# Output projection of the last eight token chunks as 2x2 block products with seven products per pair

## The chip, the cores and the metric

The kernel runs on one core of a Trainium2 chip. The metric is device time in microseconds of one execution, the median of three runs. The core has TensorE (PE in the profile; its weight loads are the row PEld), VectorE (DVE), ScalarE (ACT), GpSimd (POOL) and the queue engine SyncE (SP), which issues nearly all DMAs.

## What is computed

One encoder layer on 2048 tokens of width 1024, in fp32. The input is projected once; half of the columns feed a bidirectional gated linear attention (GLA), the other half a latent attention (MLA) with a dense softmax; the outputs of both, 512 columns each, are gated, put side by side and go through one output projection, a residual and a layer norm:

```python
def hybrid_mixer(x, positions, w_in, ..., w_out):
    h = x @ w_in
    ...
    o_a = gla_branch(g_q, g_k, g_v, g_gate, g_lr_f, g_lr_b, ...)
    o_b = mla_branch(m_cq, m_ckv, m_kr, m_gate, positions, ...)
    return jnp.concatenate([o_a, o_b], axis=-1) @ w_out

x = layer_norm(DEEPNORM_ALPHA * x + mixed, ln_g, ln_b)
```

The change concerns `@ w_out`, a product of 2048x1024 by 1024x1024, and the residual and norm behind it.

## The kernel before

All products keep fp32 accuracy by splitting each operand into a rounded high part ("hi", made by ScalarE, line L370) and a remainder ("lo", line L376, by GpSimd or VectorE). `mm3` (L422) then adds three matmuls: high by high (L424), high by low (L425), low by high (L426).

The tokens are cut into 16 chunks of 128. The program has three stages. **Sweep A** (`sweep_a`, 21.75 us per step) does the first half of the input projection and GLA chunk by chunk, **sweep C** the rest of the projection and the other scan direction. **Attention** (`attention`) goes over 16 blocks of 128 queries, transposed so that queries lie on the free axis. The order of its instructions is written out as a table of places (`PLACE`, `PLACE_OUT`): every step of each block is put at a place, all are sorted by it, and `in_order` makes each engine keep that order.

The **output projection** (`OutProj`) is the end of the program. The eight row blocks k of w_out, each 128x1024, are fetched, split and kept in SBUF (`W[k]`, tiles woh and wol). For a chunk c:

- `load` issues four DMAs of 256 KB: the GLA half of the row block (`of` from oa_s), its MLA half (`of` from ob_s) and two factors for the MLA half, the gate (`gr` from gm_s) and the reciprocal softmax sum (`gr` from r_s, broadcast over partitions). There are two `gr` tiles, used in turn.
- `gate` multiplies the MLA half by both factors on GpSimd (two operations of 128x512), `hi` and `lo` split both halves into oh and ol.
- `product` makes 48 matmuls of 128x512: two halves n of the columns, eight k, three matmuls each. The results stand in PSUM: odd chunks in a tile of two banks (po), even ones in two single banks (pmb, px).
- `residual` reads a bank with VectorE (L1983: alpha times x plus the product) and takes statistics (L1984); `finish` forms mean and variance (L1992, L1993), the normalisation by VectorE in two halves (L1995), six small ScalarE operations for the reciprocal root (L1997 to L2002), scale and shift (L2004) and two output stores (L2005).

The product of the last chunk is made by `last_product` in pieces of 512, 256 and 256 columns, so that reading can follow closely. Chunks 0 to 3 are interwoven with the last attention blocks; from chunk 4 on the order is that of the loop at the end of `attention`: in pass c the residual input of the next chunk is fetched, chunk c+2 is split, chunk c+4 loaded and chunk c multiplied and finished. Four steps of the last query block stand inside it: behind chunk 5's product its softmax sums (sx on TensorE, `rc` on VectorE), behind chunk 7's product the transposed reciprocals (`turn`: rt on TensorE, in the bank ap), the last value product (`y`, in the bank o) and their ScalarE copies (`rows`, `yc`) with stores to r_s and ob_s, from which chunks 12 to 15 are loaded.

Of the kernel before, what the change touches and what calls it, by code (L numbers as in the profile page):

```python
# [18 lines left out]
P = 128  # L19
S = 2048  # L20
# [16 lines left out]
LATE_GATES = (NCH - 1, NCH - 2, 0)  # L37
STORE_POOL = (0, 1)
# [86 lines left out]
    sum=(38.16, 49.19),  # L125
)
# [233 lines left out]
class K:  # L360
# [138 lines left out]
    def run(self):  # L499
        tc, nc, ins = self.tc, self.nc, self.ins  # L500
        with ExitStack() as top:
# [12 lines left out]
            self.ob_s = [dp.tile([P, H, QB], F32, name=f"ob_s{b}") for b in range(NQB)]  # L514

# [26 lines left out]
            rp = top.enter_context(tc.tile_pool(name="res", bufs=1, side="right", reuse_waits="tile"))  # L542
            self.ckvT_h = rp.tile([P, NKT, P], F32R, name="ckvT_h")
            self.ckvT_l = rp.tile([P, NKT, P], F32R, name="ckvT_l")
            self.kr = rp.tile([P, NKT, P], F32R, name="krs")
            self.vh = rp.tile([P, NKT, P], F32R, name="vh")
            self.vl = rp.tile([P, NKT, P], F32R, name="vl")
# [64 lines left out]
    def sweep_a(self):  # L612
        tc, nc, ins, cp = self.tc, self.nc, self.ins, self.cp
        with ExitStack() as ctx:
# [55 lines left out]
            g1 = ctx.enter_context(tc.tile_pool(name="g1", bufs=1))  # L670

# [7 lines left out]
            def step(i, steps):  # L679

                def after(g, k):
                    for n, d in steps.get((g, k), ()):
                        run(n, i if d == "cur" else i - 1)
                for g in range(3):
                    for k in self.products(ch[i], g, after):
                        pass
                    after(g, NK - 1)
                if i and ch[i]["c"] not in LATE_GATES:
                    for k in self.gate_products(ch[i]["c"], *ch[i]["x"], ip):
                        after(3, k)  # L690
                    self.gate_end(ch[i]["c"], g1)
# [17 lines left out]
            for i in range(4, NCH):  # L709
                if ch[i]["c"] > 0:  # L710
# [89 lines left out]
    def ga_x(self, i):  # L800
# [7 lines left out]
        self.lo(xl[:, :, 0], xf, xh[:, :, 0], "dve" if i < 4 else "pool")  # L808
# [228 lines left out]
    def ga_av(self, d):  # L1037
# [9 lines left out]
        nc.scalar.activation(oi, Op[:, :, 1], AF.Copy)  # L1047
# [5 lines left out]
    def ga_state(self, d):  # L1053
# [20 lines left out]
        if c > 0:  # L1074
            G.tensor_tensor(Sb[up], Sb[up], Us[up], ALU.add)
# [20 lines left out]


# [428 lines left out]
    def attention(self):  # L1526
# [4 lines left out]
        with ExitStack() as ctx:  # L1531
# [262 lines left out]
            for c, o in enumerate(first):  # L1794
# [4 lines left out]
                put(end + out["gate"][c], op.gate, o)  # L1799
            for c in range(2):  # L1800
# [26 lines left out]

            with fixed():
# [16 lines left out]
            for c in range(4, NCH):  # L1845
                with fixed():
                    if 4 < c < NCH - 1:
                        op.load_res(rest[c + 1])
                    split(c + 2)
                    load(c + 4)  # L1850
                    op.product(rest[c])
                    op.finish(rest[c])
                with self.after(*last.values()), fixed():
                    for f in {4: (tot, oh, ol), 5: (tsum, rcp), 7: (turn, y, rows, yc)}.get(c, ()):
                        f(nb - 1)


class OutProj:
# [3 lines left out]
    def __init__(self, kern, ctx, qp, bp, sp, ps, pa, pb, pc, pd):  # L1862
# [3 lines left out]
        self.raw, self.W, self.gr = {}, {}, {}  # L1866
# [24 lines left out]
    def load_ln(self):  # L1891
        self.ln = [self.slot(n) for n in ("lng", "lnb")]
        for t, n in zip(self.ln, ("ln_g", "ln_b")):
            self.nc.sync.dma_start(t, self.k.ins[n].rearrange("p (a d) -> p a d", a=2))

# [35 lines left out]
    def banks(self, o):  # L1931

        c = o["c"]
        if c < 2 or c % 2:
# [12 lines left out]
    def product(self, o):  # L1947
        if o["c"] == NCH - 1:
            return self.last_product(o)
# [8 lines left out]

    def last_product(self, o):

        c = o["c"]
        tiles = [self.ps.tile([P, 2, 512], F32, tag="pS", name=f"po{c}")[:, 0]]
        tiles += [p.tile([P, 512], F32, tag=t, name=f"p{t}{c}") for p, t in self.single[2:]]
        o["rr"] = self.bp.tile([P, 2, 512], F32, tag="ph", name=f"rr{c}", bufs=3)
        o["bn"] = self.sm.tile([P, 3, 6], F32, tag="bn3", name=f"bn{c}")
        f2 = lambda t: t.rearrange("p a d -> p (a d)")
        for i, cs in enumerate((slice(0, 512), slice(512, 768), slice(768, 1024))):
            ps = tiles[i][:, :cs.stop - cs.start]
            for k in range(NK):
                wh, wl = self.W[k]  # L1970
                self.k.mm3(ps, o["oh"][k // 4][:, k % 4], o["ol"][k // 4][:, k % 4], wh[:, cs], wl[:, cs],
                           start=(k == 0), stop=(k == NK - 1))
            rr = f2(o["rr"])[:, cs]
            self.nc.vector.scalar_tensor_tensor(rr, f2(o["xr"])[:, cs], ALPHA, ps, ALU.mult, ALU.add)
            self.nc.vector.bn_stats(o["bn"][:, i], rr)
# [10 lines left out]
    def finish(self, o):  # L1986
        kern, nc, sm = self.k, self.nc, self.sm
# [6 lines left out]
        for n in range(2):  # L1994
            V.scalar_tensor_tensor(rr[:, n], rr[:, n], mv[:, 0:1], self.ln[0][:, n], ALU.subtract, ALU.mult)  # L1995
# [6 lines left out]
        Ac.activation(rs, t, AF.Copy, scale=y)  # L2002
        for n in range(2):
            V.scalar_tensor_tensor(rr[:, n], rr[:, n], rs, self.ln[1][:, n], ALU.mult, ALU.add)  # L2004
# [69 lines left out]
```

## Time and profile before

| | |
|---|---|
| median of three runs | 1290.73 us (1290.65 to 1293.42) |
| profiled execution | 1291.78 us, span 1290.0 us |
| granted TensorE clock | 0.999 |
| chunk 4's product begins | 1149.4 us |
| chunk 8's product begins | 1194.24 us |
| last matmul | 1281.5 us |
| end of the span | 1290.0 us |

The span runs from the first to the last instruction; the 1.78 us between it and the execution's time lie around it. A row of the timeline gives the start, the duration, engine, line, operation, result and operands, shape, count, and in brackets the idle time ahead of it with what ended it. The durations of matmuls are latencies that overlap; the distance between two starts is what one costs. In DMA rows of SP the duration is the time to issue; the landing comes later.

### The profile page before, as it was taken

To read this page: it belongs to the slowest core of one execution; us is meant where nothing else is said; L and a number is where in the kernel's file an instruction comes from. 1 tells how busy PE (TensorE), PEld (TensorE's weight loads), DVE (VectorE), ACT (ScalarE), POOL (GpSimd) and SP (SyncE) were. 2 spreads that over 40 slices of the span, in tenths; PEclk is the share of its full clock that TensorE was granted. 3 is DMA by queue.
4 is the path that set the end of the run, shared out by engine and by line. 5 is a ranking of instruction groups with operands and counts; after the bars stand their busy time and mean duration, and the time that the engine had idled before them with its cause. 6 is when DMAs were issued, how large, how long until landed. Compare 5 with 4: busy or idle time off the path is not lost.

```text
span 1290.0 us, 19998 instructions
## 1 busy us (share of the span) xinstructions
PE 1265.4 (98%) x6988; PEld 1118.1 (87%) x6988; DVE 921.0 (71%) x1678; ACT 840.9 (65%) x1482; POOL 791.2 (61%) x500
## 2 busy tenths in 40 slices
PE   7999999999999999999999999999999999999997
PEld 7999998999889999999788888888888888888886
DVE  6865665555675555555898888888888889469655
ACT  7765656555676556655688888888888888523221
POOL 0243232232567666671288888889999999946550
PEclk9999999999999999999999999999999999999999
DMA  8232322232565555565401111122223110367752
GB/s 288 73 92 58 91 58 76 65 84 65 190 216 181 187 196 180 194 213 167 138 1 41 42 41 41 41 58 61 63 74 104 45 42 9 123 204 234 240 171 73
DMA packets 113444, 145.81 MB, mean 113 GB/s; under 512 B 17494, under 2 KB 70110, under 8 KB 113344
## 3 DMA queue, kind: packets, MB, share of 16 engines
q1 hardware_dynamic: 105184, 142.42, 35.3%
q0 software_dynamic: 768, 2.10, 0.5%
q8 instruction: 55, 0.90, 0.3%
q10 hardware_dynamic: 7392, 0.03, 0.3%
q14 instruction: 45, 0.37, 0.1%
HBM read 94.14 MB, written 50.36 MB: 112 GB/s over the span
## 4 chain that ended last, share of the span: by engine, by line
PE 87%; ACT 3%; DVE 2%; POOL 2%; issue 1%; DMA 1%; SPq 0%; DVEq 0%; ACTq 0%; POOLq 0%
PE o L426 4%; PE o L424 4%; PE pS L1560 4%; PE o L425 4%; PE pS L1561 4%; PE pS L1562 4%; PE pS L1563 4%; PE pS L1564 4%; PE ipa L424 3%; PE ipa L426 3%; PE ipa L425 3%; PE pz L425 2%; PE po L426 2%; PE po L425 2%; PE po L424 2%; PE pz L424 2%
## 5 line engine op out<-in xcount | busy, mean ns | idle before, releaser
L376 POOL TENSOR_TENSOR pl<-s,ph 128x1024 fp32r<-128x1024 f32 x128 | 306.1, 2415 | 56.7 <-ACT ph L370 56.7
L1582 DVE TENSOR_TENSOR rm<-pS,rm 128x512 f32<-128x512 f32 x210 | 144.7, 689 | 26.5 <-ACT s L1569 20.9
L1606 DVE TENSOR_TENSOR s<-s,mb 128x1024 f32<-128x1024 f32 x128 | 151.1, 1212 | 9.4 <-PE mb L1600 9.3
L1569 ACT ACTIVATE s<-pS 128x1024 f32<-128x1024 f32 x128 | 131.2, 1025 | 37.8 <-PE pS L1564 33.7
L370 ACT ACTIVATE ph<-s 128x1024 fp32r<-128x1024 f32 x128 | 134.9, 1057 | 13.5 <-PE o L426 12.9
L1610 ACT ACTIVATE s<-s 128x1024 f32<-128x1024 f32 x128 | 131.4, 1050 | 13.4 <-DVE s L1606 13.3
L424 PE MATMUL ipa<-wah,xah 128*128 128x384 f32 (+1 forms) x384 | 129.9, 338 | 6.7 <-ACT wah L370 6.7
L1069 POOL TENSOR_TENSOR Us<-Us,cw 128x512 f32<-128x512 f32 x16 | 18.6, 1163 | 181.7 <-DVE Us L1067 166.2
L425 PE MATMUL ipa<-wal,xah 128*128 128x384 f32 (+1 forms) x384 | 124.7, 325 | 0.2 <-DVE wal L376 0.2
L426 PE MATMUL ipa<-wah,xal 128*128 128x384 f32 (+1 forms) x384 | 124.7, 325 | 0.0
L1560 PE MATMUL pS<-qh,ckvT_h 128*128 128x512 f32 x256 | 102.5, 401 | 0.8 <-DVE rm L1582 0.4
L424 PE MATMUL o<-ph,vh 128*128 128x512 f32 x256 | 101.1, 395 | 0.0
L1561 PE MATMUL pS<-ql,ckvT_h 128*128 128x512 f32 x256 | 99.9, 390 | 0.0
L1562 PE MATMUL pS<-qh,ckvT_l 128*128 128x512 f32 x256 | 99.9, 390 | 0.0
L1563 PE MATMUL pS<-rh,krs 128*128 128x512 f32 x256 | 99.9, 390 | 0.0
L1564 PE MATMUL pS<-rl,krs 128*128 128x512 f32 x256 | 99.8, 390 | 0.0
L426 PE MATMUL o<-ph,vl 128*128 128x512 f32 x256 | 99.8, 390 | 0.0
L425 PE MATMUL o<-pl,vh 128*128 128x512 f32 x256 | 99.7, 389 | 0.0
L1633 DVE TENSOR_TENSOR ap<-ap,s 128x512 f32<-128x512 f32 x120 | 83.1, 693 | 3.5 <-ACT s L1610 0.8
L424 PEld LDWEIGHTS ipa<-wah,xah 128*128 128x128 f32 x384 | 72.9, 190 | 7.6 <-ACT wah L370 7.0
L376 POOL TENSOR_TENSOR ol<-of,oh 128x512 fp32r<-128x512 f32 x32 | 43.4, 1356 | 53.2 <-ACT oh L370 53.2
L424 PE MATMUL pz<-xch,wzh 128*128 128x256 f32 x256 | 74.8, 292 | 0.0
(327 smaller groups left out, 3836.9 us busy)
## 6 DMA issues: line engine op xcount, KB each, us to landing
xcf<-xT_dram SPq DMA_DIRECT2D x16, 512.0 KB, 4.8
xr<-x_dram SPq DMA_DIRECT2D x16, 512.0 KB, 5.8
out_dram<-rr SPq DMA_DIRECT2D x32, 256.0 KB, 4.5
xaf<-xT_dram SPq DMA_DIRECT2D x14, 512.0 KB, 3.8
oib<-oi_s SPq DMA_DIRECT2D x16, 256.0 KB, 3.9
qdb<-qd_s SPq DMA_DIRECT2D x16, 256.0 KB, 5.3
SU<-su_s SPq DMA_DIRECT2D x16, 256.0 KB, 4.7
ub<-u_s SPq DMA_DIRECT2D x16, 256.0 KB, 4.2
```

The costliest lines, as they stand in the source:

```text
L370: return nc.scalar.activation(dst, src, AF.Copy).ins
L376: return e.tensor_tensor(dst, src, hi.bitcast(F32), ALU.subtract).ins
L424: mm(out, ah, bh, start=start, stop=False)
L425: mm(out, ah, bl, start=False, stop=False)
L426: mm(out, al, bh, start=False, stop=stop)
L1560: mm(ps[:, e], kh, qh, start=True, stop=False)
L1561: mm(ps[:, e], kh, ql, start=False, stop=False)
L1562: mm(ps[:, e], kl, qh, start=False, stop=False)
L1563: mm(ps[:, e], kr, rh, start=False, stop=False)
L1564: mm(ps[:, e], kr, rl, start=False, stop=True)
L1582: V.tensor_tensor(d["rm"], src[:, e], d["rm"], ALU.max)
L1606: V.tensor_tensor(s, s, d["mb"][:, None, :].to_broadcast([P, 2, QB]), ALU.subtract)
```

## The change

Chunks 8 to 15 are taken two at a time (class `Pair`). Rows 0 and 1 of the block matrix A are the two chunks (the odd one is row 0), its columns the GLA and the MLA half; B is w_out cut into four blocks of 512x512. Instead of eight block products of 128x512x512 (96 matmuls) the pair makes seven (84 matmuls) in Winograd's form, with the sums

- S1 = A21 + A22, S2 = S1 - A11, S3 = A11 - A21, S4 = A12 - S2 of the tokens (four VectorE operations per pair),
- T1 = B12 - B11, T2 = B22 - T1, T3 = B22 - B12, T4 = B21 - T2 of the weights.

The products are P1 = A11 B11, P2 = A12 B21, P3 = S4 B22, P4 = A22 T4, P5 = S1 T1, P6 = S2 T2, P7 = S3 T3, each into a bank of its own (four single banks in turn). P1 and P7 are also copied by ScalarE, and VectorE adds the copies to P6 in PSUM (U2, U3), then reads each result out of several banks:

```diff
+    product=dict(P1=0.0, P5=2.72, P6=5.44, P3=8.16, P7=10.88, P2=13.6, P4=16.32),
+    last=dict(P1=0.0, P5=2.72, P6=5.44, P3=8.16, P2=10.88, P7=13.6, P4=16.32),
...
+    def add(self, n):
+        out, x, y, f = dict(S1=lambda: (self.s1, a21, a22, ALU.add), S3=lambda: (a21, a11, a21, ALU.subtract),
+                            S2=lambda: (a11, self.s1, a11, ALU.subtract), S4=lambda: (a11, a12, a11, ALU.subtract))[n]()
+        self.nc.vector.tensor_tensor(out, x, y, f)
...
+    def weights(self, n, k):
+        if n in ("P5", "P6", "P7"):
+            return self.op.wt(dict(P5=1, P6=2, P7=3)[n], k)
+        wk, cs = dict(P1=(k, 0), P2=(k + 4, 0), P3=(k + 4, 1), P4=(k, 1))[n]
+        return [w[:, cs * 512:(cs + 1) * 512] for w in W[wk]]
...
+    def copy(self, ps):
+        self.nc.scalar.activation(self.cp, ps(), AF.Copy)
+    def sum(self, ps):
+        self.nc.vector.tensor_tensor(ps(), ps(), self.cp, ALU.add)
+    def read(self, r, n, ps, first, cs=slice(0, 512)):
+        rr = o["rr"][:, n, cs]
+        if first:
+            self.nc.vector.scalar_tensor_tensor(rr, o["xr"][:, n, cs], ALPHA, ps(), ALU.mult, ALU.add)
+        else:
+            self.nc.vector.tensor_tensor(rr, ps(), rr, ALU.add)
...
+        for n, r, h, x, first in (("R1", 0, 0, 0, True), ("R5", 1, 1, 1, True), ("R6", 0, 1, 3, True), ("R5b", 0, 1, 1, False),
+                                  ("R2", 0, 1, 2, False), ("R3", 1, 1, 2, False), ("R7", 0, 0, b["P2"], False),
+                                  ("R4b", 1, 0, 2, last)) + (() if last else (("R4", 1, 0, 3, True),)):
```

**Weights.** In steps 4 to 14 of sweep A, 16 blocks of w_out (128x512, 256 KB) are loaded, 16 subtractions made on GpSimd (behind its Sb addition, and ahead of xal), 16 roundings on ScalarE (behind its oi copy), 16 remainders on GpSimd, and 32 stores of 256 KB to DRAM. Attention fetches them back: T1 and the high part of T2 (3 MB) behind the last scores, into tiles whose last reader has gone; the low part of T2 and the high part of T3 (2 MB) behind chunk 5's residual input; the low part of T3 (1 MB) at chunk 6; T4 (2 MB) behind chunk 7's product, over the right halves of the first four weight blocks.

```diff
+        w = self.wt[k, t] = self.cb.tile([P, 512], F32, tag="raw", name=f"wb{t}_{k}", bufs=4)
+        n = 512 * (int(t[1]) - 1)
+        self.nc.sync.dma_start(w, self.ins["wO"][k + 4 * (int(t[0]) - 1)][:, n:n + 512])
...
+        with self.after(self.oi_act):
...
+                    self.hi(h, wt[k, n[1]])
+                    self.nc.sync.dma_start(self.wt_s[int(n[1])][0][:, k], h.bitcast(F32))
...
+        with self.after(self.sb_last):
...
+                    i = G.tensor_tensor(wt[k, "1"], b["12"], b["11"], ALU.subtract)
...
+                    i = G.tensor_tensor(t, wt[k, n[1]], halves.pop(0).bitcast(F32), ALU.subtract)
+                    self.nc.sync.dma_start(self.wt_s[int(n[1])][1][:, k], t.bitcast(F32))
...
+        with self.after(*([self.wt_last] if hasattr(self, "wt_last") else [])):
+            self.lo(xl[:, :, 0], xf, xh[:, :, 0], "dve" if i < 4 else "pool")
...
+            for j, t in enumerate(("1h", "1l", "2h")):
+                put(end + 1.2 + 0.01 * j, op.fetch_t, t)
...
+                op.fetch_t("2l")
+                op.fetch_t("3h")
...
+            put(1.0, op.fetch_t, "3l")
+            put(21.9, op.fetch_t, "4h")
+            put(21.91, op.fetch_t, "4l")
```

**Chunks 6 and 7.** From chunk 6 on the order comes from places again. The four steps of the last query block that stood behind chunk 7's product now stand at 5.4 to 6.5 us after chunk 6's start, between its two halves of columns. Chunk 7 uses the banks o and ap. ln_g and ln_b are copied by ScalarE into PSUM, and the SBUF tiles that held them (named lng and lnb) become the row blocks `of` of pairs 1 and 3, so DMAs into "lnb" and "lng" are loads of chunks 10 and 11. The norm is divided in `finish_a` and `finish_b`, with the same operations.

```diff
+            for place, f in ((5.4, turn), (5.41, y), (6.5, rows), (6.51, yc)):
+                put(place, f, nb - 1)
+            put(2.0, op.ln_psum, 0)
+            put(3.5, op.ln_psum, 1)
...
-                    for f in {4: (tot, oh, ol), 5: (tsum, rcp), 7: (turn, y, rows, yc)}.get(c, ()):
...
     def banks(self, o):
+        if c == PAIR0 - 1:
+            return [p.tile([P, 512], F32, tag=t, name=f"p{t}{c}") for p, t in self.single[2:]]
...
-    def last_product(self, o):
```

On GpSimd, where chunks 8 and 9 were split, the rows were (of is the row block, gr its factors, oh and ol the parts):

```order
L376 TENSOR_TENSOR ol8_0_12931<-of8_12738,oh8_0_12929 128x512
L1916 TENSOR_TENSOR of8_12738<-of8_12738,gr4_12583 128x512 x2
L376 TENSOR_TENSOR ol8_1_12937<-of8_12738,oh8_1_12935 128x512
L376 TENSOR_TENSOR ol9_0_13025<-of9_12838,oh9_0_13023 128x512
L1916 TENSOR_TENSOR of9_12838<-of9_12838,gr5_12593 128x512 x2
L376 TENSOR_TENSOR ol9_1_13031<-of9_12838,oh9_1_13029 128x512
```

Now they are, for pair 0 (chunks 9 and 8), with the last digit of a name the pair's number:

```order
L1996 TENSOR_TENSOR of9_12988<-of9_12988,gr5_12739 128x512 x2
L398 TENSOR_TENSOR A11l0_13159<-of9_12988,A11h0_13117 128x512
L398 TENSOR_TENSOR S1l0_13222<-s1_0_13197,S1h0_13202 128x512
L398 TENSOR_TENSOR S2l0_13228<-of9_12988,S2h0_13224 128x512
L1996 TENSOR_TENSOR lnb_12572<-lnb_12572,gr4_12729 128x512
L398 TENSOR_TENSOR S3l0_13264<-of8_12888,S3h0_13261 128x512
L1996 TENSOR_TENSOR lnb_12572<-lnb_12572,gr4_12729 128x512
L1996 TENSOR_TENSOR lng_12571<-lng_12571,gr5_12739 128x512 x2
L398 TENSOR_TENSOR A22l0_13320<-of8_12888,A22h0_13268 128x512
L398 TENSOR_TENSOR A12l0_13338<-of9_12988,A12h0_13259 128x512
L398 TENSOR_TENSOR S4l0_13344<-of9_12988,S4h0_13266 128x512
```

The gates of the next pair's chunks (lnb, lng) stand ahead of the last three remainders of this pair. On ScalarE the copies rt15 and yc15 stood behind chunk 7's norm:

```order
L2001 ACTIVATE ln7_t_13101<-ln7_w_13102 128x1
L2002 ACTIVATE ln7_r_13103<-ln7_t_13101,ln7_y_13100 128x1
L1711 ACTIVATE rt15_13120<-rt15_13114 4x128
L1734 ACTIVATE yc15_13123<-y15_13116 128x512
L370 ACTIVATE oh10_0_13128<-of10_12939 128x512
```

They now stand behind chunk 5's norm, the two copies of the norm's vectors and the first rounding of pair 0:

```order
L2263 ACTIVATE ln5_r_13058<-ln5_t_13056,ln5_y_13055 128x1
L2144 ACTIVATE ln0_13112<-lng_12571 128x1024
L2144 ACTIVATE ln1_13115<-lnb_12572 128x1024
L392 ACTIVATE A11h0_13117<-of9_12988 128x512
L1783 ACTIVATE rt15_13153<-rt15_13119 4x128
L1806 ACTIVATE yc15_13156<-y15_13121 128x512
L392 ACTIVATE S1h0_13202<-s1_0_13197 128x512
```

They moved from two chunks later, and have a row ahead of them that reads chunk 9's load. At the end of VectorE's order (pw0 to pw3 are the single banks, xr holds the sum of a row block), behind the last whole bank of the pair, it now says:

```order
L2036 TENSOR_TENSOR pw2_13274<-pw2_13274,pc3_14009 128x512
L2044 TENSOR_TENSOR xr14_13793<-pw2_13274,xr14_13793 128x512
L2042 SCALAR_TENSOR_TENSOR xr14_13793<-xr14_13793,pw2_13274 128x512
L2044 TENSOR_TENSOR xr14_13793<-pw3_13275,xr14_13793 128x256
L2050 BN_STATS bn14_14027<-xr14_13793 128x6 x2
L2269 SCALAR_TENSOR_TENSOR xr15_13770<-xr15_13770,ln15_r_13990,ln1_13115 128x512 x2
L2044 TENSOR_TENSOR xr14_13793<-pw0_13272,xr14_13793 128x256
```

The last row reads the last quarter of the result; before, nothing of another chunk stood between the last pieces.

More of the change, by code (lines that the diff above doesn't have):

```diff
@@ L514, in run @@
             self.ob_s = [dp.tile([P, H, QB], F32, name=f"ob_s{b}") for b in range(NQB)]
+            self.wt_s = {j: [dp.tile([P, 4, 512], F32, name=f"wt{j}{p}_s") for p in "hl"] for j in range(1, 5)}
             ident = cp.tile([P, P], F32, name="ident")
@@ L709, in sweep_a @@
             for i in range(4, NCH):
+                for k, t in WT_LOADS.get(i, ()):
+                    self.wt_load(k, t)
                 if ch[i]["c"] > 0:
@@ L1826, in split @@
                     op.lo(rest[c], 1)
+            pairs = [Pair(op, p, PAIR0 + 2 * p + 1, PAIR0 + 2 * p) for p in range((NCH - PAIR0) // 2)]
             with fixed():
@@ new lines, in attention @@
+            for place, f in ((5.4, turn), (5.41, y), (6.5, rows), (6.51, yc)):
[5 more added lines that the diff above has]
+            put(21.91, op.fetch_t, "4l")
+            for q in pairs:
+                q.put(put, 4 * half + PAIR_US * q.p, q is pairs[-1])
+            for _, _, fn, a in sorted(todo, key=lambda e: e[:2]):
+                with self.in_order(late):
+                    fn(*a)
```

239 lines of the change are left out of this document (205 added, 34 removed).

## The prediction

> **What bounds the kernel now.** I read the page first: the busy shares and the chain of work that ended last.
>
> ```profile
> PE 1265.4 (98%) x6988; PEld 1118.1 (87%) x6988; DVE 921.0 (71%) x1678; ACT 840.9 (65%) x1482; POOL 791.2 (61%) x500
> PE 87%; ACT 3%; DVE 2%; POOL 2%; issue 1%; DMA 1%; SPq 0%; DVEq 0%; ACTq 0%; POOLq 0%
> ```
>
> TensorE is busy for 98% of the span and is 87% of the chain, so matmuls that go are worth time where they are issued back to back. The list of what TensorE waited for, from 1080 us to the end (total, times, longest), and the busy time by stretches (PE, PEld, DVE, ACT, POOL, then clock, DMA share, GB/s) say that they are:
>
> ```profile
> PE y L424 <- DVE rc L1692: 0.3, 1, 0.3
> 1170.00:1180.00 10.00, 10.00 (x47) 8.05 (x46) 8.24 (x15) 3.02 (x9) 7.84 (x6) 1.00 0.40 118
> 1190.00:1200.00 10.00, 10.00 (x46) 8.15 (x45) 9.62 (x14) 3.44 (x11) 6.39 (x5) 1.00 0.91 318
> 1205.10:1226.88 21.78, 21.78 (x97) 18.02 (x97) 13.42 (x20) 5.30 (x16) 10.68 (x9) 1.00 0.70 224
> ```
>
> There is one wait of 0.3 us in 210 us, at clock 1.00. But look at the neighbours: VectorE has 9.62 of 10 us filled and the DMA engines a share of 0.91 at 1190, just where the pairs are prepared. TensorE is never late only because everything is ahead of it; the change puts more on all of them and gives them less time.
>
> **The matmuls that go.** The timeline of TensorE, first matmul of chunk 8, first of chunk 9, and two of the last quarter:
>
> ```profile
> 1194.24 0.39 PE L424 MATMUL pmb<-woh,oh 128*128 128x512 f32 x1
> 1205.14 0.39 PE L424 MATMUL po<-woh,oh 128*128 128x512 f32 x1
> 1281.37 0.28 PE L425 MATMUL pap<-wol,oh 128*128 128x256 f32 x1
> 1281.49 0.28 PE L426 MATMUL pap<-woh,ol 128*128 128x256 f32 x1
> ```
>
> 48 matmuls take 10.90 us, 0.2271 each (the 0.39 is latency, not pitch). A pair has 84 instead of 96: 4 x 12 x 0.2271 = 10.90 us. The narrow matmuls (pitch 0.12) are 24 instead of 48, and each two cost 0.24 against 0.227: 0.16 more. **-11.06 us.**
>
> **Sweep A.** Eleven steps get three operations each on GpSimd (the last one two), up to three roundings on ScalarE, and DMAs of 256 KB.
>
> ```profile
> 307.25 2.39 POOL L376 TENSOR_TENSOR xal<-xaf,xah 128x1024 fp32r<-128x1024 f32 x1 [3.29 <-ACT xah L370]
> 304.25 0.60 ACT L1516 ACTIVATE gs<-ipg 128x512 f32<-128x512 f32 x1 [2.20 <-PE ipg L426]
> 281.75:303.50 21.75, 21.75 (x139) 20.73 (x138) 11.75 (x23) 12.76 (x28) 6.83 (x6) 1.00 0.26 73
> PE Ap L425 <- DVE qbl L376: 1.1, 1, 1.1
> ```
>
> The new work stands in the gap of 3.29 us on GpSimd (three operations of about 1.3, so 0.6 too much) and in that of 2.20 us on ScalarE (three of about 0.6). DMAs use 0.26 of the engines. What may be late is xal, by about 1 us, and the lines of VectorE beside it; TensorE waited there once for qbl, 1.1 us. Value **+0.3**, bounds 0 and 1.5. The three fetches of 1 MB after the last scores have SP's empty stretch to themselves:
>
> ```profile
> 1057.00 30.64 SPq L1735 DMA_DIRECT2D ob_s<-yc  x2
> 1098.89 0.33 SPq L1873 DMA_DIRECT2D wof<-wO_dram  x1
> ```
>
> From 1087.6 to 1098.9 there are 11.3 us; 3.1 MB at the 318 GB/s above take 9.9. Nothing is charged; without that cover it would be about 1 us on a weight that is needed much later.
>
> **The softmax row moved into chunk 6.** It now stands behind the first half of chunk 6, which ends where px begins; it needs rc.
>
> ```profile
> 1177.11 0.39 PE L424 MATMUL px<-woh,oh 128*128 128x512 f32 x1
> 1179.89 0.18 DVE L1694 RECIPROCAL rc<-rc 128x4 f32<-128x4 f32 x1
> ```
>
> rc is done at 1180.07; TensorE is there at 1177.11 and stands still: **+3.0**. VectorE's order up to there is unchanged, so I see nothing that brings rc forward; two fetches of 1 MB, ahead of the output stores whose buffers VectorE reuses, may delay it (bounds 2.5 and 4.5).
>
> **Chunk 7's banks.** Chunk 7 now uses the o and ap banks, which hold rt and y until ScalarE has copied them; on ScalarE the copies stand behind A11h0, and that waits for chunk 9's first transfer. Its issue, the median landings between 1160 and 1215 us, and the copies as they are now:
>
> ```profile
> 1182.66 0.33 SPq L1907 DMA_DIRECT2D of<-oa_s  x1
> 1184.28 0.53 SPq L1910 DMA_DIRECT2D of<-ob_s  x1
> of<-oa_s SPq DMA_DIRECT2D x6, 256.0 KB, 3.9
> of<-ob_s SPq DMA_DIRECT2D x6, 256.0 KB, 7.5
> 1198.18 0.25 ACT L1711 ACTIVATE rt<-rt 4x128 f32<-4x128 f32 x1
> 1198.34 0.57 ACT L1734 ACTIVATE yc<-y 128x512 f32<-128x512 f32 x1
> ```
>
> Landing 1186.6, A11h0 about 0.6, copies 0.7: 1187.9. TensorE ends chunk 6 at 1180.07 + 0.81 (rt and y) + 5.45 = 1186.3. **+1.6**, bounds 0.5 and 3. Behind yc stands the store of ob_s, and behind that on SP, also behind 1 MB of wt3, are the loads of pair 1: 1188 instead of 1189.78 for chunk 10 today, yet now two chunks at once.
>
> **The fourth product of pair 0 (P3) waits for S4l0.** On GpSimd S4l0 stands behind the gates of chunk 11, so pair 0 waits for pair 1's load. Gates (two at a time) and remainders cost:
>
> ```profile
> 1177.39 2.66 POOL L1916 TENSOR_TENSOR of<-of,gr 128x512 f32<-128x512 f32 x2
> 1191.48 3.44 POOL L1916 TENSOR_TENSOR of<-of,gr 128x512 f32<-128x512 f32 x2
> 1195.67 1.29 POOL L376 TENSOR_TENSOR ol<-of,oh 128x512 fp32r<-128x512 f32 x1 [0.74 <-ACT oh L370]
> 1180.79 1.84 POOL L376 TENSOR_TENSOR ol<-of,oh 128x512 fp32r<-128x512 f32 x1 [0.74 <-ACT oh L370]
> ```
>
> Chunk 9's last part lands at 1184.28 + 7.5 = 1191.8, its gates end at 1194.5 to 1195.2; only then are chunk 11's gate buffers free. Its ob_s goes out 1.2 later, at 1195.7 to 1196.4, lands 7.5 later at 1203.2 to 1203.9, is gated by 1205.9 to 1207.3, and A22l0, A12l0, S4l0 (3 x 1.29 to 1.84) end at 1209.8 to 1212.8. TensorE begins pair 0 at 1187.9 + 10.9 = 1198.8 and is at P3 36 matmuls later, 1207.0. That is 2.8 to 5.8 us; the extra 1.3 MB (wt3, ob_s) in the queue is worth another 4.1 at 318 GB/s, and a landing like that of oa_s (3.9) would leave nothing. I take **+5.0**, bounds 0 and 10.
>
> Pair 1: its P3 is due at 1198.8 + 19.08 + 5.0 + 8.2 = 1231.1. Chunk 13's slot comes free with S4l0 near 1212; eight issues (4.3), 7.5, gates 3.1 and three remainders 4.2 give 1231.1 too: **+1.0**, bounds 0 and 4. Later pairs have an emptier queue.
>
> **VectorE in the pairs.** The groups between 1205 and 1248.6, which hold four chunks (busy total, mean ns), and the longest such row of the tail:
>
> ```profile
> L2004 DVE SCALAR_TENSOR_TENSOR rr<-rr,ln_r,lnb 128x512 f32<-128x512 f32 x8 | 9.8, 1264 | 1.6 <-ACT ln_r L2002 1.6
> L1995 DVE SCALAR_TENSOR_TENSOR rr<-rr,mv,lng 128x512 f32<-128x512 f32 x8 | 5.6, 745 | 0.0
> L1983 DVE SCALAR_TENSOR_TENSOR rr<-xr,px 128x512 f32<-128x512 f32 x2 | 1.4, 686 | 6.5 <-PE px L426 6.5
> 1190.23 3.54 DVE L2004 SCALAR_TENSOR_TENSOR rr<-rr,ln_r,lnb 128x512 f32<-128x512 f32 x2
> ```
>
> Two SBUF inputs cost 1.264 beside GpSimd, one SBUF and one PSUM input 0.69. Two chunks cost 13.42 today. Five more reads of banks (3.4), two sums (1.4) and four adds of 0.69 to 1.26 (2.8 to 5.0) come on top; ln_b and ln_g in PSUM take off 4 x 0.57 + 4 x 0.06 = 2.5. That is 18.5 to 20.7 us a pair, against 19.08 us of matmuls: level. **+1.0**, bounds 0 and 6 (4 x 1.6).
>
> The groups say that a VectorE operation with two SBUF inputs is stretched beside GpSimd by 0.57 in the mean, and the last row by 1.08 (3.54 for two). [...]
>
> **The end.** Today the last quarter's read starts as soon as TensorE is done.
>
> ```profile
> 1281.81 0.42 DVE L1974 SCALAR_TENSOR_TENSOR rr<-xr,pap 128x256 f32<-128x256 f32 x1 [2.00 <-PE pap L426]
> 1284.87 1.42 DVE L2004 SCALAR_TENSOR_TENSOR rr<-rr,ln_r,lnb 128x512 f32<-128x512 f32 x2 [0.40 <-ACT ln_r L2002]
> ```
>
> Afterwards VectorE has R4b's bank read, half a's read, two statistics and the second half of chunk 15's norm in front of it: 0.69 + 0.42 + 0.69 + 0.43 + 1.4, from 1.44 us before the last matmul, so 1.5 to 2 us late; U3 before them waits for a ScalarE copy behind chunk 15's norm chain, which makes 3.2 possible. **+2.5**, bounds 1 and 4.
>
> **Sum.** -11.06 + 0.3 + 3.0 + 1.6 + 5.0 + 1.0 + 1.0 + 2.5 = +3.3 us on the profiled execution of 1291.78 us (span 1290.0), so 1295.1. That execution was 1.05 above the median of 1290.73; set against the median this is **1294 us**. The gain is real and is eaten by waits.
>
> **Rivals.**
> - *Loads land in time* (the other side). If chunk 11's parts land within about 4 us, S4l0 is there before P3, and VectorE keeps level: the two waits and VectorE's term vanish, -11.06 + 0.3 + 3.0 + 1.6 + 2.5 = -3.7, 1287, and 1283 with the small terms at their low ends. For it: the DMA share falls to 0.70 after 1205. Against it: 0.91 at 1190. It decides at S4l0 before 1207. 0.30.
> - *VectorE is the bound*: if each add is stretched as the worst row (1.77), a pair takes 15.7 + 4 x 1.77 = 22.8 instead of 19.08, 3.7 x 4 = 14.8 us in place of the 1.0 and of the 6 for P3: +3.3 - 1.0 - 6.0 + 14.8 = +11.1, 1302. [...] For it: 9.62 of 10 at 1190. Against: one-SBUF-input operations are untouched. 0.17.
> - *All covered:* rc or the copies come earlier than today's rows allow: -11, 1280. 0.05.
>
> The forecast has 0.48 (1288 to 1300 by its own bounds). The range 1284 to 1302 leaves out most of the third rival and the upper part of the second. A difference of 0.2% (2.6 us) is about what a measurement of this kernel tells from none: faster 0.33 (the first and third, nearly), within 0.17 (the low part of the forecast), slower 0.50.
>
> **What would show it.** Right: TensorE waits for rc (3), for a ScalarE copy before chunk 7 (1.6), for S4l0 (5), and the span ends over 10 us after the last matmul, not 8.4. Wrong: no wait for S4l0; chunk 11's gates done before 1203; VectorE under 9 of 10 us in the pairs; or new TensorE waits in sweep A above 1.5 us.

## The result and the profile after

The changed kernel takes **1293.87 us** (median of 20 runs, 1292.57 to 1295.88) against 1291.68 for the kernel before in as many runs: a ratio of **1.0017, interval 1.0011 to 1.0024**. It is slower by 2.2 us, just inside what I called no difference, and 0.1 us from the forecast (the kernel before took 0.95 longer here than in the runs that the forecast started from; the difference, 2.2, stands against a forecast of 3.3). Its profiled execution took 1292.98 us, the span 1291.2.

The page of the changed kernel, the same two lines as before:

```profile
PE 1258.6 (97%) x6928; PEld 1112.4 (86%) x6928; DVE 955.1 (74%) x1722; ACT 862.1 (67%) x1520; POOL 845.4 (65%) x544
PE 76%; DVE 6%; POOL 4%; DMA 3%; ACT 3%; issue 3%; SPq 1%; DVEq 0%; POOLq 0%; ACTq 0%
```

TensorE has 60 matmuls fewer (48 by the product, and 12 because fewer are cut into two narrow ones) and is busy for 6.8 us less, but its share of the chain that ended last fell from 87% to 76%: VectorE and GpSimd now stand on it with 6% and 4%. The list of what TensorE waited for, from 1080 us to the end (total, times, longest), says where:

```profile
PE rt L1777 <- DVE u L2254: 2.6, 1, 2.6
PE pw L448 <- POOL S4l L398: 2.5, 1, 2.5
PE pw L446 <- DVE xr L2044: 0.8, 1, 0.8
PE y L446 <- DVE rc L1764: 0.3, 1, 0.3
```

One wait has become four. The timeline of TensorE at the first one shows a second loss, which the list of waits cannot show:

```profile
1176.74 0.39 PE L448 MATMUL pmb<-woh,ol 128*128 128x512 f32 x1
1179.68 0.27 PE L1777 MATMUL rt<-ident,rc 128*4 128x128 f32 x1 [2.56 <-DVE u L2254]
...
1181.29 0.63 PE L447 MATMUL px<-wol,oh 128*128 128x512 f32 x1
1181.72 0.63 PE L448 MATMUL px<-woh,ol 128*128 128x512 f32 x1
```

Ahead of the wait the matmuls last 0.39 us; behind it 0.63, and they start 0.427 us apart instead of 0.227. The busy time by stretches (PE, PEld, DVE, ACT, POOL, then clock, DMA share, GB/s) shows this as a clock of 0.59, and again behind the wait for S4l:

```profile
1179.68:1183.80 4.12, 4.12 (x12) 3.30 (x13) 4.12 (x4) 3.70 (x9) 2.79 (x2) 0.59 0.94 339
1211.00:1214.40 3.40, 3.40 (x10) 2.60 (x9) 3.15 (x4) 1.67 (x3) 2.11 (x2) 0.54 1.07 345
```

TensorE is "busy" in all of both stretches; only the clock column (0.59 and 0.54) tells that it does half the work. Each has eight matmuls at the slow pitch, so each loses 8 x 0.20 = 1.6 us. The load of the DMA engines is not what slows it, since between the two stretches it runs at full speed beside a share as high:

```profile
1190.00:1200.00 10.00, 10.00 (x45) 8.26 (x44) 8.36 (x12) 4.73 (x12) 7.75 (x7) 1.00 1.10 350
```

The granted clock of the whole execution is 0.994. In all 20 executions it lay between 0.993 and 0.996, against 0.996 to 0.999 in 35 of the kernel before that were run beside the experiments, so the stretches are probably not those of this one execution alone; they can't be counted this way, since the end, where TensorE stands idle, lowers the clock too (0.57 from 1281 to 1291 us).

The same view with the cuts at the first matmul of each pair and after the last matmul:

```profile
1198.41:1221.86 23.45, 20.99 (x85) 16.86 (x84) 19.59 (x30) 8.15 (x20) 19.66 (x15) 0.93 1.02 338
1221.86:1240.90 19.04, 19.04 (x85) 15.76 (x84) 18.56 (x28) 7.50 (x19) 13.27 (x11) 1.00 0.65 202
1240.90:1261.07 20.17, 19.36 (x86) 15.69 (x84) 19.59 (x33) 8.05 (x21) 13.76 (x11) 1.00 0.33 123
1261.07:1280.14 19.07, 19.07 (x96) 16.27 (x95) 16.44 (x30) 5.57 (x20) 1.47 (x2) 1.00 0.15 56
```

Two pairs run at the speed of their 84 matmuls (19.08 us); the first takes 4.4 us longer, the third 1.1. VectorE is filled for 18.6 to 19.6 us of every pair but the last. In the first pair GpSimd is filled too (19.66 of 23.45) and the DMA engines have a share of 1.02.

The last matmul of the changed kernel:

```profile
1280.14 0.28 PE L448 MATMUL pw<-woh,A22l 128*128 128x256 f32 x1
```

It starts 1.35 us sooner than before. **The balance:** -11.06 for the matmuls, +2.7 at rc, +2.6 at S4l, 2 x 1.6 for the half-speed stretches behind them, +1.0 in the third pair, +0.1 before chunk 6 is -1.5, as measured within 0.2. From the end of the last matmul's 0.12 us to the end of the span are 10.9 us instead of 8.4: +2.5. So the span is 1.2 us longer. The eleven microseconds came, and were given back piece by piece.

### The profile page after: what moved, and what is told of

Read it like the earlier page. It is cut to its first block, busy times and chain, and to the rows that moved or that the text cites. A ratio compares the mean times of both kernels' runs of the same rounds, so it can differ in the third digit from the quotient of the medians.

```text
span 1291.2 us, 20146 instructions
## 1 busy us (share of the span) xinstructions
PE 1258.6 (97%) x6928; PEld 1112.4 (86%) x6928; DVE 955.1 (74%) x1722; ACT 862.1 (67%) x1520; POOL 845.4 (65%) x544
## 4 chain that ended last, share of the span: by engine, by line
PE 76%; DVE 6%; POOL 4%; DMA 3%; ACT 3%; issue 3%; SPq 1%; DVEq 0%; POOLq 0%; ACTq 0%
PE pS L1632 4%; PE pS L1634 4%; PE pS L1635 4%; PE pS L1633 4%; PE pS L1636 4%; PE o L446 4%; PE o L447 4%; PE o L448 4%; PE ipa L446 3%; PE ipa L448 3%; PE ipa L447 3%; PE pz L447 2%; PE pz L446 2%; PE pz L448 2%; PE ipg L446 2%
## 5 line engine op out<-in xcount | busy, mean ns | idle before, releaser
L1095 POOL TENSOR_TENSOR Us<-Us,cw 128x512 f32<-128x512 f32 x16 | 18.6, 1163 | 174.1 <-DVE Us L1093 158.6
L447 PEld LDWEIGHTS ipa<-wal,xah 128*128 128x128 f32 x384 | 73.6, 192 | 0.6 <-DVE wal L398 0.2
```

The source lines that it names most:

```text
L447: mm(out, ah, bl, start=False, stop=False)
```

## The experiments

The theory after the result: TensorE's gain is real, and what eats it is single waits at named places (rc, S4l, the end), plus the half speed behind the longer ones. The rivals: VectorE's amount of work is the bound, whatever the waits; or the waits are one shortage that only moves when one of them is taken away. All ratios are against the kernel before on the same chip.

### The weights alone

The kernel before with sweep A's loads, combinations, roundings and stores added; nothing reads them.

```diff
+WT_LOADS = {4: ((0, "11"), (0, "12"), (0, "22")), ...}
+WT_STEPS = {4: "t1.0 t3.0 t2.0", 5: "s1.0 s3.0 t4.0", ...}
...
+                    if i in WT_STEPS:
+                        self.wt_work(WT_STEPS[i])
...
+                for k, t in WT_LOADS.get(i, ()):
+                    self.wt_load(k, t)
```

> The kernel before with only sweep A's part of the change: the 16 loads, 16 subtractions, 16 roundings, 16 remainders and 32 stores of the weight combinations, which nothing reads afterwards. Theory: all of it lies in gaps, 0 to 0.5 us. Rival (the steps of sweep A are stretched, or the stores delay its loads): 1.5 us or more, and new waits of TensorE before 350 us.

Measured: 1291.68 us, ratio 1.0003 (0.9993 to 1.0012), span 1289.9, no new wait of TensorE. The combinations made in the first sweep cost nothing that can be measured.

### The softmax row alone

The kernel before with turn, y, rows and yc between the two halves of chunk 6; then with one, and with two of the second half's weight blocks ahead of them, so that TensorE comes to rt later.

```diff
-                    op.product(rest[c])
-                    op.finish(rest[c])
+                    if c == 6:
+                        for k in range(NK):
+                            op.part(rest[c], k, (0,))
+                        op.residual(rest[c], 0)
+                        for k in range(0):
+                            op.part(rest[c], k, (1,))
...
-                    for f in {4: (tot, oh, ol), 5: (tsum, rcp), 7: (turn, y, rows, yc)}.get(c, ()):
+                    for f in {4: (tot, oh, ol), 5: (tsum, rcp), 6: (turn, y, rows, yc)}.get(c, ()):
```

> The kernel before with one part of the change alone: softmax row and value product (with their copies) between the two halves of chunk 6, nothing else; chunk 7 keeps its banks. Theory: TensorE waits 2.6 to 3.0 us for rc, and the matmuls after that run at half speed for about 4 us, which costs 1.7 more; nothing hides it: 4.3 to 4.7 us slower than before (1.0035). Rival 1 (the half speed in the changed kernel has another cause, such as the extra DMA traffic): 2.6 to 3.0 us slower and no slow stretch.

> The same, one weight block later (3 matmuls, 0.68 us): the wait for rc becomes about 2.0 us. If any idle stretch of 2 us lets the clock fall, some 3.7 us slower than before; if it takes 2.4 us or more, 2.0.

> The same, two weight blocks later: the wait becomes about 1.3 us. Expected without a slow stretch, since the changed kernel's wait of 0.8 us in pair 2 had none: 1.3 us slower than before; with one, 3.0.

The first of them, the wait and the stretch behind it:

```profile
PE rt L1705 <- DVE u L2006: 2.4, 1, 2.4
```

```profile
1179.70:1183.80 4.10, 4.10 (x19) 3.40 (x20) 4.10 (x4) 2.37 (x8) 2.79 (x2) 1.00 0.93 316
```

Ratios 1.0038 (1.0021 to 1.0054), 1.0021 (1.0012 to 1.0031) and 1.0017 (1.0007 to 1.0027) with waits of 2.4, 2.0 and 1.5 us. In the profiled executions the moved row costs what it waits: the last matmul is 2.6, 2.6 and 3.2 us later than in the kernel before, where chunk 6 already began 0.2, 0.5 and 1.8 us later. None of the three has a slow stretch: 19 matmuls in the 4.1 us above, where the changed kernel had 12, and clock 1.00. That is what the rival had expected of the first kernel. Its median says more: the whole interval (2.7 to 7 us on 1291.8) lies above the 2.6 us. Its profiled execution, 1294.35, was the shortest of its six, and the others reach 1300.66; the granted clock was 0.998 in it and 0.995 in the longest. It may be that some of them had the slow stretch, which the profile of one execution cannot say.

### Chunk 11's gates behind pair 0's work

S4l0 stands behind the gates of chunk 11 on GpSimd. Here the gates of the next pair are placed later, behind it.

```diff
-    gate=((-19.94, -18.58), (-24.72, -21.3)),
+    gate=((-14.3, -14.2), (-14.5, -14.4)),
```

> The changed kernel with one edit: on GpSimd the gates of the next pair stand behind the last remainder (S4l) of this pair instead of ahead of its last three. Theory: pair 0's fourth product waits for S4l only because S4l is queued behind chunk 11's load; the wait of 2.5 us goes, and with it the stretch of half-speed matmuls behind it (about 1.7 us), so TensorE ends 3 to 4 us earlier, 1290 us or less, and the wait that is left is VectorE's. Rival 1 (S4l is late by its own inputs, since VectorE and ScalarE are full): the wait stays above 1.5 us and the time within 1 us of the changed kernel. Rival 2 (the slow matmuls have to do with the DMA load and not with the wait): the wait goes, the slow stretch between 1211 and 1214 us stays.

Measured: 1293.45 us, ratio 1.0013 (1.0005 to 1.0022), span 1292.1. The waits of TensorE from 1080 us on:

```profile
PE pw L446 <- DVE xr L2044: 3.9, 2, 3.6
PE rt L1777 <- DVE u L2254: 2.6, 1, 2.6
PE po L446 <- ACT yc L1806: 0.7, 1, 0.7
```

The wait for S4l is gone, so the gates were its cause. But one of 3.6 us stands in its place, at P2 of the same pair, whose bank VectorE must have read. VectorE's timeline ahead of it:

```profile
1207.66 1.76 DVE L2008 TENSOR_TENSOR s<-lnb 128x512 f32<-128x512 f32 x1 [0.39 <-POOL lnb L1996]
1209.45 1.67 DVE L2008 TENSOR_TENSOR lnb<-lng,lnb 128x512 f32<-128x512 f32 x1
1212.30 1.73 DVE L2008 TENSOR_TENSOR lng<-s,lng 128x512 f32<-128x512 f32 x1 [1.18 <-POOL A11l L398]
...
1215.26 1.42 DVE L2044 TENSOR_TENSOR xr<-pw,xr 128x512 f32<-128x512 f32 x2
```

The read of the bank (L2044) stands behind the next pair's adds (L2008). Those now wait for a gate that was moved (0.39 us) and for A11l (1.18), which GpSimd makes behind the gates, and last about 1.7 us each. Removing the wait on one engine gave it to the next engine in the row, through an instruction that needs nothing from the gates.

The stretches behind the two longer waits:

```profile
1180.50:1184.60 4.10, 4.09 (x19) 3.42 (x20) 4.10 (x4) 3.70 (x9) 3.47 (x3) 1.00 0.98 331
1216.00:1220.40 4.40, 4.39 (x13) 3.50 (x14) 3.96 (x6) 1.36 (x3) 2.44 (x3) 0.65 1.10 315
```

After 2.56 us at rt the clock stays up, though the same 2.56 us pulled it down in the changed kernel; after 3.60 it falls. And with chunk 6 at full speed TensorE now comes to the o bank too early: the wait for yc of 0.7 us that I had forecast (1.6) and that the changed kernel did not show. The 3 to 4 us that I had expected did not come; the last matmul, at 1280.98 us, is no sooner than in the changed kernel.

### The row later

The softmax row, with its reads and ln_b and ln_g, moved behind five of the eight weight blocks of chunk 6's second half, the two halves of 6 and 7 spread so that it fits, and A11's parts of pair 0 behind it.

```diff
-                        put(t + half * n, op.part, o, k, (n,))
+                        put(t + half * n + 0.68 * k, op.part, o, k, (n,))
...
-            for place, f in ((5.4, turn), (5.41, y), (6.5, rows), (6.51, yc)):
+            for place, f in ((8.7, turn), (8.71, y), (8.8, rows), (8.81, yc)):
...
-            put(2.0, op.ln_psum, 0)
-            put(3.5, op.ln_psum, 1)
+            put(9.0, op.ln_psum, 0)
+            put(9.1, op.ln_psum, 1)
...
-            at(P_["hi"][n], self.hi, n)
-            at(P_["lo"][n], self.lo, n)
+            a = (n, self.p) == ("A11", 0)
+            at(-12.1 if a else P_["hi"][n], self.hi, n)
+            at(-12.0 if a else P_["lo"][n], self.lo, n)
```

> The changed kernel with one part moved: the softmax row's transposition and the value product stand five weight blocks into the second half of chunk 6 (3.4 us later), their ScalarE copies ahead of the first rounding of pair 0 and of the two copies of the norm's vectors. Theory: the wait for rc (2.6 us) goes, and the half-speed stretch behind it (1.7 us); chunk 7 starts about 4 us earlier. Of that, part comes back at S4l, which hangs on chunk 11's load and that on GpSimd's gates of chunk 9, which do not move: its wait grows from 2.5 to 4 to 6 us. So the time falls by 0 to 2 us only, against 4.4 if the two waits were independent. Rival (the copies delay chunk 7): a wait for ScalarE of over 1 us before chunk 7.

Measured: 1294.32 us, ratio 1.0024 (1.0015 to 1.0032). What TensorE waits for:

```profile
PE pw L448 <- POOL S4l L398: 7.1, 1, 7.1
PE pw L446 <- DVE xr L2044: 0.8, 1, 0.8
```

The wait for rc is gone and its half speed with it. The wait for S4l has grown by nearly all that was won, from 2.5 to 7.1 us (I had expected 4 to 6), since GpSimd is hardly earlier: S4l begins at 1207.49 us here and at 1207.89 in the changed kernel. The slow stretch behind it is longer as well, 13 matmuls, 2.6 us. Neither repair is worth anything alone.

### Both, and the end

Both edits together; then, on top, the last pair's steps in another order: ScalarE's copy of P7 earlier (c7), and chunk 15's last scale and shift (the first of fb) later, so that it no longer stands ahead of the read of the last quarter.

```diff
-    read_last=dict(..., R7=13.7, bn11=14.3, c7=16.4,
-                   U3=17.1, R3=17.7, bn22=17.8, R4b=17.71, fa=(14.9, 20.0), fb=(17.9, 24.0)),
+    read_last=dict(..., R7=13.7, bn11=14.3, c7=14.85,
+                   U3=17.1, R3=17.7, bn22=17.8, R4b=17.71, fa=(14.9, 20.0), fb=(20.1, 24.0)),
```

> Both edits together: gates behind S4l, softmax row later. Theory: both waits and both half-speed stretches go, TensorE ends 6 to 8 us before the changed kernel's 1280.3, less what VectorE then holds up (it is filled 9.7 of 10 us in the pairs): 1285 to 1289 us, faster than the kernel before. Rival (the bound is VectorE all the same): the waits for S4l and rc go, but waits for VectorE of 4 us or more come instead, and the time stays above 1290.

> As the one before, and the end rearranged: the ScalarE copy of P7 ahead of chunk 15's norm chain, and the scale and shift of chunk 15 behind the last quarter's reading and chunk 14's first normalisation. Theory: the 10.9 us from the last matmul to the end become 9.5 to 10 (8.4 before the change), so 1 us below the one before. Rival (VectorE's queue is as long whatever its order): no difference.

Measured: 1293.76 us, ratio 1.0013 (1.0005 to 1.0022), and 1292.11, ratio 1.0004 (0.9995 to 1.0012). In both the waits are these:

```profile
PE pw L446 <- DVE xr L2044: 6.1, 2, 5.6
PE pw L448 <- POOL S4l L398: 0.9, 1, 0.9
```

```profile
PE pw L446 <- DVE xr L2044: 6.1, 2, 5.6
PE pw L448 <- POOL S4l L398: 0.8, 1, 0.8
```

With rc and S4l nearly out of the way the first pair stands 5.6 us at P2, and matmuls at half speed follow in both. I had expected 1285 to 1289 us of the first kernel; what came is its rival, waits of VectorE of 4 us or more. So far the waits behave as one shortage that moves. The end behaved as a term of its own: 9.8 us from the last matmul (1280.92) to the end of the span instead of 10.9, and 1.65 us in the median.

### The next pair's adds behind the bank's read

In the kernel with the later gates, and in the one with all three repairs, the adds S1, S3 and S2 of the next pair, with the roundings and remainders of S1 and S2, are placed behind the read that P2 waits for.

```diff
-    add=dict(S1=-10.55, S3=-9.85, S2=-9.15, S4=-4.37),
-    hi=dict(A11=-17.26, S1=-9.75, S2=-8.35, ...),
-    lo=dict(A11=-13.14, S1=-8.45, S2=-7.09, ...),
+    add=dict(S1=-6.95, S3=-6.9, S2=-6.85, S4=-4.37),
+    hi=dict(A11=-17.26, S1=-6.8, S2=-6.7, ...),
+    lo=dict(A11=-13.14, S1=-6.75, S2=-6.65, ...),
```

> As the run with the gates behind S4l, and on VectorE the next pair's three adds S1, S3, S2 (with their roundings and remainders) placed behind the read of the bank that the sixth product P2 needs, instead of ahead of this pair's sums and reads. Theory: with the gates moved, the adds waited for them and the bank's read stood behind the adds (wait of 3.6 us at P2); that wait goes, and no wait above 1 us is left in the pairs, only the one of 2.6 us for rc: TensorE's last matmul near 1276 to 1278, the time 1288 to 1290. Rival (VectorE has too much work per pair in any order): waits for VectorE of 3 us or more remain, spread over the pairs, and the time stays at 1292 or above.

> Everything together: softmax row later, gates behind S4l, adds behind the read, end rearranged. Theory: no wait above 1 us and no half-speed stretch between 1160 us and the end; last matmul 1271 to 1274, 9.5 to 10 us from there to the end, 1282 to 1286 us, 0.5% faster than the kernel before. Rival as before: waits for VectorE of 3 us or more remain and the time stays above 1289.

Measured: 1295.63 us, ratio 1.0032 (1.0019 to 1.0045), and 1293.28, ratio 1.0014 (1.0005 to 1.0023). This theory fell: I had expected both below the kernel before. What TensorE waits for VectorE in the second kernel, and the stretch from 1215 to 1235 us:

```profile
PE pw L446 <- DVE xr L2044: 6.0, 6, 1.3
```

```profile
1215.00:1235.00 20.00, 17.99 (x78) 14.06 (x77) 19.29 (x31) 7.28 (x20) 12.25 (x11) 1.00 0.70 223
```

One wait of 5.6 us became six of up to 1.3, two in each of the last three pairs (with one of 0.9 us for S4l and one of 0.6 for a copy of ScalarE in or behind the first), and the pairs take 21.2 to 21.9 us. No matmul runs at half speed. VectorE's timeline before one of the six, and TensorE's first matmul behind it:

```profile
1231.72 1.75 DVE L2008 TENSOR_TENSOR of<-s,of 128x512 f32<-128x512 f32 x1
...
1235.55 1.76 DVE L2008 TENSOR_TENSOR of<-of 128x512 f32<-128x512 f32 x1 [0.74 <-POOL S2l L398]
1237.23 0.69 DVE L2036 TENSOR_TENSOR pw<-pw,pc 128x512 f32<-128x512 f32 x1
...
1239.29 0.67 DVE L2044 TENSOR_TENSOR xr<-pw,xr 128x512 f32<-128x512 f32 x1
```

```profile
1240.02 0.50 PE L446 MATMUL pw<-wt1h,S1h 128*128 128x512 f32 x1 [1.19 <-DVE xr L2044]
```

P5 of the next pair needs the bank whose read (1239.29) ends behind two adds that last 1.75 us each and behind a wait for GpSimd. VectorE is filled for 19.3 of 20 us here, so two causes are possible: too much work, or its order. The kernel with all three repairs, without the edit of this section, makes the same operations. Its second pair, and the second pair with the edit:

```profile
1223.00:1242.04 19.04, 19.04 (x86) 15.77 (x84) 18.49 (x30) 7.43 (x19) 12.26 (x10) 1.00 0.63 204
```

```profile
1214.04:1235.92 21.88, 19.87 (x85) 15.64 (x85) 20.62 (x32) 7.94 (x21) 14.13 (x12) 1.00 0.73 229
```

The last three pairs take 19.04, 19.80 and 19.08 us without the edit, 21.88, 21.70 and 21.72 with it. So it is the order that brings these waits. It also makes VectorE's work longer: 20.62 us in the pair above instead of 18.49; the add S4 takes 1.75 to 1.77 us in the first three pairs with the edit, against 0.68 to 0.69 in three of the four pairs of the changed kernel.

### Amount or order

The kernel with all repairs once without the last scale and shift of chunks 8 to 15, which takes 2 x 1.4 us of VectorE out of every pair; and once, from the kernel with both repairs and the end, with the adds S1 and S3 made by GpSimd right behind the gates, and S2 and S4, with their roundings and S2's remainder, placed later on VectorE.

```diff
-            nc.vector.scalar_tensor_tensor(rr[:, n], rr[:, n], o["rs"], self.ln[1][n], ALU.mult, ALU.add)
+            if c < PAIR0:
+                nc.vector.scalar_tensor_tensor(rr[:, n], rr[:, n], o["rs"], self.ln[1][n], ALU.mult, ALU.add)
```

```diff
-    add=dict(S1=-10.55, S3=-9.85, S2=-9.15, S4=-4.37),
-    hi=dict(A11=-17.26, S1=-9.75, S2=-8.35, ..., S4=-3.53, ...),
-    lo=dict(A11=-13.14, S1=-8.45, S2=-7.09, ...),
+    add=dict(S1=-14.1, S3=-14.05, S2=-2.5, S4=-0.9),
+    hi=dict(A11=-17.26, S1=-9.75, S2=-2.40, ..., S4=-0.80, ...),
+    lo=dict(A11=-13.14, S1=-8.45, S2=-2.30, ...),
...
-        self.nc.vector.tensor_tensor(out, x, y, f)
+        (self.nc.gpsimd if n in ("S1", "S3") else self.nc.vector).tensor_tensor(out, x, y, f)
```

> As the run with everything together, and the last scale and shift of chunks 8 to 15 left out (two VectorE operations of 0.7 us a chunk, 2.8 us a pair; the normalised values are stored without them). In that run a pair takes 21.7 us instead of 19.05, with two waits for VectorE in each. Theory: VectorE's work is what a pair takes; with 2.8 us less of it the pairs come down to 19.0 to 19.5 us, the waits to under 0.6 each, the last matmul to 1272 to 1275, and the end is 2 us shorter as well. Rival (the waits come from the order of VectorE's work and from GpSimd, on which it waits, not from the amount): the pairs stay above 20.5 us.

> The version that the runs point to, with nothing left out: softmax row later, gates behind S4l, end rearranged; S1 and S3 of the next pair added by GpSimd right behind its gates instead of by VectorE, and VectorE's S2 and S4 put behind its reads of the banks that TensorE needs next. Theory: VectorE gives up 1.4 to 3.4 us a pair, GpSimd takes 2.6 (16.9 of 19.05), so neither is the bound: pairs of 19.1 to 19.6 us, no wait above 1.5 us, last matmul 1271 to 1275, the time 1282 to 1287, faster than both kernels. Rival (GpSimd becomes the bound, or its two adds slow VectorE's operations with two SBUF inputs as much as they relieve it): pairs above 20 us, the time at 1290 or above.

Measured: 1289.34 us, ratio 0.9983 (0.9974 to 0.9993), with less work; and **1288.07, ratio 0.9974 (0.9963 to 0.9984)**, with all of it. The first kernel, 1235 to 1255 us, and its waits for VectorE:

```profile
1235.00:1255.00 20.00, 18.94 (x82) 15.04 (x82) 17.23 (x27) 7.25 (x21) 13.85 (x11) 1.00 0.41 142
```

```profile
PE pw L446 <- DVE xr L2044: 4.2, 6, 1.3
```

VectorE has 2.8 of 20 us free and TensorE still waits for it, up to 1.3 us at a time; the pairs take 20.7 to 22.3 us, as the rival had put it. So less work alone does not take the waits away. The second, in the same stretch and in its first pair:

```profile
1195.00:1215.00 20.00, 16.87 (x72) 13.37 (x73) 15.31 (x23) 8.91 (x21) 19.77 (x17) 1.00 1.05 348
1235.00:1255.00 20.00, 20.00 (x90) 16.57 (x89) 19.31 (x32) 8.69 (x22) 17.25 (x14) 1.00 0.65 221
```

From 1235 to 1255 us VectorE is filled for 19.31 of 20 us and TensorE for 20.00 of 20 at clock 1.00: a full VectorE need not hold TensorE up. This run changes the amount and the order at once, so it does not say what each is worth. Its pairs take 23.30, 20.06, 19.04 and 19.08 us, those of the kernel that it starts from 28.53, 19.04, 19.80 and 19.08, so nearly all that it gains lies in the first pair, where the wait of 5.6 us and the half speed behind it are gone. The last matmul starts at 1275.58 us, the span is 1285.5. This version beats both kernels. It remains 1 us above the range that I had expected: GpSimd is full in its first pair (19.77 of 20), where TensorE still waits 3.9 us, among them 1.6 for A11l and 1.4 for S4h.

## Why the prediction was right, point by point

The time and the sign were right, and five of the eight terms within 0.3 us. But three terms came out too large and one was missing, and these cancelled in part.

- **Matmuls, -11.06:** right. Two pairs take 19.04 and 19.07 us, the last included, and the balance closes with this number.
- **Sweep A, +0.3:** nothing. Chunk 6 starts at 1171.42 us instead of 1171.36, and the weights alone cost 0.0003 of the time (interval through zero).
- **rc, +3.0:** 2.7. The cause is shown: the row alone brings the wait (2.4) and its time into the kernel before, and the row later takes it away. VectorE's order did stay, as argued: the row that releases TensorE is at 1179.36, half a microsecond sooner than before.
- **Chunk 7's banks, +1.6:** no wait. ScalarE's order is as I had it, the copies behind A11h0:

```profile
1185.46 0.63 ACT L392 ACTIVATE A11h<-of 128x512 fp32r<-128x512 f32 x1 [1.92 <-DMA of<-oa_s]
1185.99 0.25 ACT L1783 ACTIVATE rt<-rt 4x128 f32<-4x128 f32 x1
1186.15 0.57 ACT L1806 ACTIVATE yc<-y 128x512 f32<-128x512 f32 x1
```

  They are done at 1186.7 and not at 1187.9, and TensorE, slowed down, came only at 1187.53 instead of 1186.3. Where the slow stretch is missing, 0.7 us of the wait appears (the kernel with the later gates). The term was hidden by another loss and too large by half.
- **S4l0 at P3, +5.0:** the mechanism as put, the size half, 2.6. GpSimd's timeline:

```profile
1202.32 2.68 POOL L1996 TENSOR_TENSOR lng<-lng,gr 128x512 f32<-128x512 f32 x2
1204.95 1.30 POOL L398 TENSOR_TENSOR A22l<-of,A22h 128x512 fp32r<-128x512 f32 x1
1206.20 1.73 POOL L398 TENSOR_TENSOR A12l<-of,A12h 128x512 fp32r<-128x512 f32 x1
1207.89 1.71 POOL L398 TENSOR_TENSOR S4l<-of,S4h 128x512 fp32r<-128x512 f32 x1
```

  Chunk 11's last issue (1195.78), its gates and the three remainders came in the order and nearly at the times of the forecast; S4l ends at 1209.6, just ahead of 1209.8 to 1212.8. On the way two slips cancelled, which is luck: chunk 9's gates ended at 1192.6, some 2 us sooner than forecast, and the issue came 3.2 us behind them, not 1.2. What was mis-sized is the further 4.1 us for 1.3 MB in the queue, of which I had taken a part: the last part landed 5.9 us after its issue, sooner than the 7.5 already in the sum.
- **Pair 1's P3, +1.0:** nothing; its 19.04 us hold no wait.
- **VectorE in the pairs, +1.0:** 1.0, one wait in the third pair. The estimate of 18.5 to 20.7 us a pair held (18.56 to 19.59). Single adds were dearer than the mean I used: beside GpSimd's operations six of the changed kernel's 16 took 1.65 to 1.76 us, two 0.95 and 1.07 and one 0.67; the seven with GpSimd idle took 0.68 to 0.69. None took longer than 1.76, while two of GpSimd's remainders beside them took 1.71 and 1.73 instead of 1.29, so both sides may lose something.
- **The end, +2.5:** 2.5, and moving one copy of ScalarE and one scale and shift took 1.1 of it back.
- **Missing:** the half speed behind the two waits, 3.2 us. The forecast treated a wait of TensorE as costing its length. Without it the sum with the measured sizes is -11.06 + 0.1 + 2.7 + 2.6 + 1.0 + 2.5 = -2.2 on the profiled execution, faster; with it +1.0, where +1.2 was measured. My sum reached +3.3 by three terms that were 5.0 too large together. The size of the result is partly luck; its mechanism, a real gain eaten by waits at rc, at S4l0 and at the end, is not.

Of the rivals, *loads land in time* failed on S4l0, which came 2.5 us too late. *VectorE is the bound* failed as a price, but its engine is the one through which the waits pass when the others are mended. *All covered* failed at rc. What stays open: how often other executions have the slow stretches, and what would take the last 3.9 us from the first pair of the kernel with GpSimd's adds. One candidate was not run: with the later gates and the later adds of S1, S3 and S2 the first pair took 19.04 us, without a wait (21.22 with all the repairs), and the other pairs got longer, so those adds could be placed later in the first pair alone.

## What to carry to other kernels

Count a saving on the busiest engine only down to the next engine's slack, and follow each in-order engine: an operation that waits for a load holds up every bank read behind it, so a wait that is taken away comes back one engine further on until the order there is changed too (here 2.5 us for GpSimd's S4l came back as 3.6 us for VectorE's read). Repairs of such a chain are tried together, since each alone may show nothing or a loss; here three were worth 1.8 us against the changed kernel and a fourth, two adds moved to another engine and two to a later place, 4 more. And a wait of a few microseconds on TensorE is priced with the half-speed matmuls that may follow (here eight behind each of the waits of 2.56 and 2.46 us, 1.6 us of loss each), which only the clock column shows.

## What the runs showed of the hardware

TensorE fell to half speed behind some waits: a pitch of 0.427 us instead of 0.227 over 8 to 13 matmuls, in stretches of about 3.4 to 5.5 us. In these traces, from 1160 us on, it did so after every idle stretch of 3.6 us or more (3.60 with the later gates, 5.64 with both repairs and again with the end, 7.05 with the later row), and after 2.46, 2.56 and 2.68 us in three places (the first two in the changed kernel, the third with the later gates and adds), but not after 2.56 and 2.37 us in two others (the later gates, the softmax row alone); after 2.04 us or less it was never seen. So the length of the wait alone does not settle it here: 2.56 us did both. What else decides it, no run here shows.
